# Hybrid SSD and attention trunk in FP32 on one core: order of copies, row splits, down products and weight units at the stage borders

## Chip, cores and metric

The kernel runs on one core of a Trainium2 chip. The metric is the device time in microseconds of one execution, as the median of three runs.

## What is computed

The reference is a bidirectional encoder trunk over 512 positions of width 1024, with two layers. Each layer adds to the residual stream `h`, in this order: half of a SwiGLU feed-forward block (width 2816), a mixer (layer 0: bidirectional Mamba-2 SSD; layer 1: two-dimensional neighbourhood attention), half of a second SwiGLU block, and a gated projection of a per-layer input. Every block normalises `h` first.

```python
def ssd_mixer(h, w_in, conv_w, conv_b, dt_bias, a_log, d_skip, norm_g, w_out):
    proj = h @ w_in
    z, xbc, dt_raw = jnp.split(proj, [SSD_D_INNER, SSD_D_INNER + SSD_CONV_DIM], axis=-1)
    xbc = jax.nn.silu(centred_depthwise_conv(xbc, conv_w, conv_b))
    ...
    y_fwd = ssd_scan(xs, dt[:, :, 0], a[0], grp(b_f), grp(c_f))
    y_bwd = flip(ssd_scan(flip(xs), flip(dt[:, :, 1]), a[1], flip(grp(b_b)), flip(grp(c_b))))
    y = (y_fwd + y_bwd + xs * d_skip[:, None]).reshape(bsz, seqlen, SSD_D_INNER)
    y = rmsnorm(y * jax.nn.silu(z), norm_g)
    return y @ w_out
...
for i in range(DEPTH):
    h = h + 0.5 * swiglu(rmsnorm(h, ffn1_norm[i]), ffn1_w_gu[i], ffn1_w_down[i])
    h = h + mixer_i(rmsnorm(h, mix_norm[i]))
    h = h + 0.5 * swiglu(rmsnorm(h, ffn2_norm[i]), ffn2_w_gu[i], ffn2_w_down[i])
    gate = jax.nn.sigmoid(rmsnorm(h, ple_norm[i]) @ ple_w_gate[i])
    h = h + gate * rmsnorm(p[i] @ ple_w_proj[i], ple_post_norm[i])
```

## The kernel before

The residual stream lies transposed in SBUF, as eight sub-blocks of 128 features by 512 positions (`h[0]` to `h[7]`). Products keep FP32 accuracy by splitting each operand into a rounded high part and the rest: one product is three matmuls, at lines 277, 280 and 281 in `gemm`. A product over eight sub-blocks is 24 matmuls of 512 columns.

**Weights as units.** A unit is a weight tile of 128 by up to 1024, loaded by a DMA (line 204), rounded on ScalarE (line 221, `wh`) and split on DVE (line 223, `wl`), with three buffers each. `plan` lists all units of the program in the order of use. `unit` (line 258) prepares units until three are ready and hands out the first. What `unit` prepares is traced before the product that asked for it.

**Order of the work.** The program text is a priority, not an order: a scheduler at build time issues on each engine what is ready, earlier text first, and hands out the buffers of a ring likewise. `tc.issue_after(ins)` keeps what a block traces on the engine of `ins` behind it.

**FFN.** The first four (in the very first FFN six) column pairs of gate and up are plain products (`gate_up`); the rest are done in blocks of seven products with halves of the columns (`block`, lines 504 to 506, 24 matmuls of 256 columns). `ffn_order` lays the down products of one chunk between the blocks of the next. `activate` multiplies gate and up and splits the result (lines 299 and 300) for the down products. The norm's sum of squares is a column sum on TensorE (`SumSq.begin`, line 342); it is placed inside the second product, after `at` of the eight sub-blocks.

**The first FFN's start.** `first` runs the first four products as loads come in, then prepares three units, and only then (behind the third unit's cast) squares the eight sub-blocks (line 324, ScalarE) and adds them (line 328, DVE).

**SSD.** Eight groups. `project(gi)` makes eight products for a group; the first six go through a convolution of five taps (`conv`: ScalarE lines 748 and 755, DVE lines 752 and 756), the last two are gates (lines 774 and 775). `scan(gi)` is a generator of eight steps that runs beside `project(gi + 1)`, one step per product. Its first step transposes four chunks (line 818), copies them out of PSUM on ScalarE (line 821) and forms the chunk products (line 829), which DVE masks (line 832). All of these use a ring of three PSUM banks (`px_bank`); the big products use a ring of five (`mm_bank`). POOL multiplies the masks in (lines 808 and 811). In the driver, the first product of the next group and its convolution stand in the text ahead of the scan's first step:

```python
for gi in range(NG):
    beside = project(gi + 1) if gi + 1 < NG else out_half()
    sn = scan(gi, *cur, e0)
    ...
    for i, r in enumerate(beside):
        ...
        while pending:
            pending.pop(0)()
        next(sn, None)
```

The last group has no next projection; the first half of the out projection (`out_half`) runs beside it. For this, eight rows of earlier groups come back from DRAM and are scaled and split: cast on ScalarE (line 302), rest on DVE (line 303). Rows 0 to 2 are split beside the last projection, 3 to 7 after the last scan's transposes. `pending` holds a group's gate product (line 926) with its square.

**Attention.** `attend(j)` runs beside `project(j + 1)`. It forms scores (line 1157), transposes the values (line 1191) and the weights (line 1200), and multiplies both (`weigh`, line 1210) into `po`, a bank of the ring of three, which ScalarE and DVE then split (lines 299 and 300).

Of the kernel before, what the change touches and what calls it, by code (L numbers as in the profile page):

```python
# [27 lines left out]
NG = 8  # L28
# [21 lines left out]
def ffn_order(chunks):  # L50

    for f in range(chunks[0][1]):
        yield "plain", f
    for c in range(1, len(chunks)):
        a, b = chunks[c]
        blocks = [(p, i) for p in range(a // 2, b // 2) for i in range(7)]
        d = 0
        for n, (p, i) in enumerate(blocks):  # L60
            yield "block", p, i
            while d < KD and (d + 0.5) * len(blocks) <= KD * (n + 1):
                yield "down", c - 1, d
                d += 1
    yield "between",
    for d in range(KD):
        yield "down", len(chunks) - 1, d
# [3 lines left out]
def trunk(ctx, tc, A, out):  # L71
# [183 lines left out]
        top_up()  # L255
        return True

    def unit():
        while len(ready) < 3 and prep_next():
            pass  # L260
        return ready.pop(0)

# [127 lines left out]
    def ffn(norm, nxt, between=None, first=None, at=4):  # L390
# [159 lines left out]
        for what, *a in ffn_order(chunks):  # L550
            if what == "plain":
                if left and R[0] is not None:
                    sums(left.pop(0))
                gate_up(a[0])
            elif what == "block":

                if between and a in ([chunks[-1][0] // 2, 0], [NF // 2 - 1, 4]):
                    next(between)
                block(*a)
            elif what == "between":  # L560
                made = between and next(between)
            else:
                c, d = a
                last = c == len(chunks) - 1
                pt = mm_bank() if last else px_bank()
                gemm(pt, unit(), [mids[f] for f in range(*chunks[c])])
                v.scalar_tensor_tensor(out=h[d], in0=pt, scalar=0.5, in1=h[d], op0=ALU.mult, op1=ALU.add)
                if last:
                    nxt(d)
                    if d in (2, 4) and made is not None:  # L570
                        made[d // 2]()
# [36 lines left out]
    def ple(l, norm, pp, nxt):  # L608
        halves = (slice(0, T // 2), slice(T // 2, T))

        def gate(n, pt, R, cs):
            if isinstance(pp[n], tuple):
                p_, r3 = pp[n]
                tc.keep_in_program_order(
                    v.scalar_tensor_tensor(out=p_, in0=p_, scalar=col(C_GQ + 8 * l + n), in1=r3, op0=ALU.mult,
                                           op1=ALU.mult))
                pp[n] = p_
            u = t2()[:, cs]
            v.tensor_mul(out=u, in0=pt, in1=R[:, cs])
            s.activation(out=u, in_=u, func=AF.Tanh)  # L620
            v.scalar_tensor_tensor(out=u, in0=u, scalar=1.0, in1=pp[n][:, cs], op0=ALU.add, op1=ALU.mult)
            v.tensor_add(out=h[n][:, cs], in0=h[n][:, cs], in1=u)

        R = None
        for n in range(KD):
            if n == KD - 1 and nxt is done:

                w = unit()
                for x, cs in enumerate(halves):
                    pt = mm_bank()  # L630
                    gemm(pt[:, cs], w, norm.pairs, cols=cs)
                    gate(n, pt[:, cs], R, cs)
                    (sy, s)[x].dma_start(out=out[:, n, cs], in_=h[n][:, cs])
                continue
            pt = mm_bank()
            gemm(pt, unit(), norm.pairs, behind=n == 0)
            if n == 0:
                norm.begin(half=True)
                held = pt
                continue  # L640
            if n == 1:
                R = norm.end()
                gate(0, held, R, slice(0, T))
                nxt(0)
            for cs in ((slice(0, T),) if n < KD - 1 else halves):
                gate(n, pt[:, cs], R, cs)
            nxt(n)


    def ssd(norm, nxt):  # L650
# [107 lines left out]
        def project(gi):  # L758
            bt, ct_, xt, zt = md(), md(), md(), md()
            cts = (16 + gi, 32 + gi, 24 + gi, 40 + gi, 2 * gi, 2 * gi + 1)  # L760
            dsts = (bt[:, 0], bt[:, 1], ct_[:, 0], ct_[:, 1], xt[:, 0], xt[:, 1])
            for i in range(8):
                raw = gi == 0 and i < 3
                if gi == 0 and i == 0:
                    pt = pt0
                else:
                    pt = mm_bank()
                    gemm(pt, unit(), norm.pairs if raw else xn)
                if i < 6:
                    conv(pt, cts[i], dsts[i], raw)  # L770
                else:

                    th = t2()
                    s.activation(out=th, in_=pt, func=AF.Tanh, scale=0.5)
                    v.scalar_tensor_tensor(out=zt[:, i - 6, :], in0=th, scalar=1.0, in1=pt, op0=ALU.add, op1=ALU.mult)
                yield bt, ct_, xt, zt
# [202 lines left out]
                held_[k] = md(F32R)  # L979
                rows[k] = row(k, held_[k])  # L980

        held_ = {}

        def pairs_of(ks):
            res = []
            for k in ks:
                pr = held_.pop(k) if k in held_ else md(F32R)
                yt = row(k, pr) if k < 14 else late[k - 14]
                split(pr, yt, col(C_SN + k))
                res.append(pr)  # L990
            return res

# [16 lines left out]
        for gi in range(NG):  # L1009
            beside = project(gi + 1) if gi + 1 < NG else out_half()  # L1010
            sn = scan(gi, *cur, e0)
            if gi == NG - 1:
                next(sn)
                prs += pairs_of(range(3, 8))
                next(sn)
            for i, r in enumerate(beside):
                cur = r
                if i == 7 and gi == NG - 2:
                    prs = pairs_of(range(3))
                while pending:  # L1020
                    pending.pop(0)()
                next(sn, None)
                if i == 5 and gi == NG - 2:
                    early_rows()
                if i == 6 and gi + 1 < NG:
                    e0 = expo(gi + 1, 0)
# [1 line left out]
        prs = pairs_of(range(8, 16))  # L1028
        ss.begin(0.5, 4.0 * EPS)
        for d in range(KD):  # L1030
            pt, w = mm_bank(), unit()
            gemm(pt, w, prs[:4], last=False)
            if d == 0:
                r2 = ss.end()
            old = sc()
            sy.dma_start(out=old, in_=hd[d])
            gemm(pt, w, prs[4:], first=False, off=4)

            h[d] = hs()
            u = t2()  # L1040
            grid = "p (r c) -> p r c"
            by_column = h[d].rearrange("p (c r) -> p r c", c=64)
            if d < KD - 1:
                v.tensor_add(out=u, in0=pt, in1=parts[d])
                v.tensor_mul(out=u, in0=u, in1=r2)
                v.tensor_add(out=by_column, in0=old.rearrange(grid, c=64), in1=u.rearrange(grid, c=64))
            else:

                v.tensor_mul(out=u, in0=parts[d], in1=r2)
                v.tensor_add(out=by_column, in0=old.rearrange(grid, c=64), in1=u.rearrange(grid, c=64))  # L1050
                w = t2()
                v.tensor_mul(out=w.rearrange("p (c r) -> p r c", c=64), in0=pt.rearrange(grid, c=64),
                             in1=r2.rearrange(grid, c=64))
                v.tensor_add(out=h[d], in0=h[d], in1=w)
            nxt(d)


    def attention(norm, nxt):
# [87 lines left out]
        def attend(j):  # L1146
# [71 lines left out]
            for x in range(2):  # L1218
                turn(2 * x)
                turn(2 * x + 1)  # L1220
                yield
            po = px_bank()
            weigh(po)
            op = opr[j] = md(F32R)
            split(op, po, None)
# [26 lines left out]
        for d in range(KD):  # L1252
            if d < 4:
                pt, w = outs[d]
                gemm(pt, w, opr[6:], first=False, off=6)
            else:
                pt = mm_bank()
                gemm(pt, unit(), opr)
            fetch(d, hd[d])
            v.tensor_add(out=h[d], in0=pt, in1=h[d])  # L1260
            nxt(d)
# [41 lines left out]
    def first(pts, pairs):  # L1303
        done_ = [0] * 4
        here, cut_ = 0, [0] * 4
        for o in order:
# [4 lines left out]
            for u in range(4):  # L1311
                while done_[u] < min(here, 4 * cut_[u]):
                    k = done_[u]
                    gemm(pts[u], begun[u][2:], pairs[k:k + 1], first=k == 0, last=k == KD - 1, off=k)
                    done_[u] += 1
        while len(ready) < 3:
            prep_next()

        with tc.issue_after(splits[-1].ins):
            for k in range(KD):  # L1320
                n.count(k, True)

    for i in range(stop):
        l, w = divmod(i, 4)
# [1 line left out]
        m = None if last else Norm(gains[i + 1], (lambda: md(F32R)) if w == 2 else xa)  # L1326
        nxt = done if last else m.prep
        if w == 0:
            ffn(n, nxt, first=first if i == 0 else None, at=7)
        elif w == 1:  # L1330
            (ssd if l % 2 == 0 else attention)(n, nxt)
        elif w == 2:
            pp = ffn(n, nxt, ple_proj(l))
        else:
            ple(l, n, pp, nxt)
# [103 lines left out]
```

## Time and profile before

| | us |
|---|---|
| runs: median (lowest to highest) | 2330.28 (2328.69 to 2330.52) |
| profiled execution, its own time | 2331.44 |
| span of the profiled execution | 2329.6 |
| TensorE matmuls, busy | 2310.9 (99%) |
| DVE busy | 1827.4 (78%) |
| ScalarE busy | 1166.6 (50%) |
| POOL busy | 323.1 (14%) |

PE is TensorE, ACT is ScalarE, PEld is the load of weights into TensorE, and SP issues the DMAs. Lines are those of the kernel before. In a list of waits each row gives who waited, for what, the sum in us, how many times, and the longest. In a timeline a row gives start, duration of the run of equal instructions, engine, line, operation, tiles and count, and in brackets the idle time before it and what ended it. In windows a row gives the stretch, its length, busy time with the count of instructions, the granted clock of TensorE as a share of full speed, and the share of the DMA engines with GB/s. TensorE's matmuls are pipelined, and their ends in the trace are modelled.

### The profile page before, as it was taken

Reading aid. Unit: us, or ns where it says so; the run is one execution under the profiler, and the core shown is the slowest. Engines: PE = TensorE matmul, PEld = TensorE weight load, DVE = VectorE, ACT = ScalarE, POOL = GpSimd, SP = SyncE. Lnnn points to the kernel's source line nnn. Section 1 sums busy time; section 2 is a strip of 40 time slices with the busy share of each in tenths; the row PEclk is TensorE's granted clock in tenths of the full one; section 3 lists DMA queues with packets and bytes.
Section 4 is the critical chain, followed back from the end, with each engine's and each line's share of the span. In section 5 each row is a group of like instructions: output and inputs, shape, how many; then the busy total and the mean of one; then the engine's idle time right before and its main releaser. Section 6 shows DMA issues by size and latency. Waiting matters only on the chain.

```text
span 2329.6 us, 35378 instructions
## 1 busy us (share of the span) xinstructions
PE 2310.9 (99%) x13798; PEld 2022.4 (87%) x13798; DVE 1827.4 (78%) x2621; ACT 1166.6 (50%) x2028; POOL 323.1 (14%) x253
## 2 busy tenths in 40 slices
PE   9999999999999999999999999999999999999999
PEld 7899998888888788899998889999878788999987
DVE  7878878888877858978875897887678859877856
ACT  5434345776666763543345444334436754343452
POOL 0000001355555551000003100000100010000020
PEclk9999999999999999999999999999999999999999
DMA  5323323444444543223323322332433233323232
GB/s 183 123 73 109 106 88 128 141 145 154 142 148 142 161 160 122 92 95 105 123 69 105 109 84 98 105 123 64 145 120 122 106 114 101 109 100 100 82 100 73
DMA packets 99240, 265.97 MB, mean 114 GB/s; under 512 B 12016, under 2 KB 12912, under 8 KB 99072
## 3 DMA queue, kind: packets, MB, share of 16 engines
q1 hardware_dynamic: 98784, 263.57, 34.3%
q8 instruction: 108, 1.77, 0.3%
q14 instruction: 60, 0.49, 0.1%
q10 hardware_dynamic: 288, 0.14, 0.0%
HBM read 253.40 MB, written 10.26 MB: 113 GB/s over the span
## 4 chain that ended last, share of the span: by engine, by line
PE 63%; DVE 1%; ACT 1%; issue 0%; DVEq 0%; ACTq 0%
PE ps L277 12%; PE ps L280 12%; PE ps L281 12%; PE ps L506 8%; PE ps L505 8%; PE ps L504 8%; PE ps L1210 1%; PE ps L1200 1%; PE ps L1191 0%; PE ps L352 0%; PE ps L1132 0%; PE ps L1157 0%; PE ps L1087 0%; PE ps L342 0%; ACT md L299 0%; DVE md L300 0%
## 5 line engine op out<-in xcount | busy, mean ns | idle before, releaser
L277 PE MATMUL ps<-md,wh 128*128 128x512 f32 (+1 forms) x2032 | 801.5, 395 | 2.0 <-ACT md L299 1.6
L280 PE MATMUL ps<-md,wh 128*128 128x512 f32 (+1 forms) x2032 | 794.4, 391 | 1.1 <-DVE md L303 1.0
L281 PE MATMUL ps<-md,wl 128*128 128x512 f32 (+1 forms) x2032 | 792.0, 390 | 1.7 <-DVE wl L223 1.7
L221 ACT CAST wh<-wr 128x1024 fp32r<-128x1024 f32 (+2 forms) x395 | 352.3, 893 | 528.5 <-issue 195.8
L223 DVE TENSOR_TENSOR wl<-wr,wh 128x1024 fp32r<-128x1024 f32 (+2 forms) x395 | 420.6, 1065 | 85.8 <-ACT wh L221 84.8
L281 PEld LDWEIGHTS ps<-md,wl 128*128 128x128 f32 x2032 | 381.7, 188 | 83.0 <-DVE wl L223 3.1
L277 PEld LDWEIGHTS ps<-md,wh 128*128 128x128 f32 x2032 | 382.3, 188 | 78.6 <-issue 2.4
L280 PEld LDWEIGHTS ps<-md,wh 128*128 128x128 f32 x2032 | 382.4, 188 | 76.5 <-issue 2.8
L221 ACT CAST wh<-md 128x1024 fp32r<-128x1024 f32 x175 | 183.5, 1049 | 318.4 <-PE ps L505 271.8
L328 POOL TENSOR_TENSOR sq<-sq,sq 128x512 f32<-128x512 f32 x71 | 102.7, 1446 | 1703.9 <-ACT sq L324 1699.3
L506 PE MATMUL ps<-sc,wl 128*128 128x256 f32 x980 | 277.4, 283 | 0.0
L506 PE MATMUL ps<-md,wl 128*128 128x256 f32 x980 | 277.3, 283 | 0.0
L505 PE MATMUL ps<-md,wh 128*128 128x256 f32 x980 | 277.3, 283 | 0.0
L505 PE MATMUL ps<-sc,wh 128*128 128x256 f32 x980 | 277.2, 283 | 0.0
L504 PE MATMUL ps<-md,wh 128*128 128x256 f32 x980 | 277.1, 283 | 0.0
L504 PE MATMUL ps<-sc,wh 128*128 128x256 f32 x980 | 276.6, 282 | 0.0
L510 DVE TENSOR_TENSOR t<-ps,t 128x512 f32<-128x512 f32 x245 | 165.7, 688 | 126.3 <-PE ps L506 123.8
L223 DVE TENSOR_TENSOR wl<-md,wh 128x1024 fp32r<-128x1024 f32 x175 | 213.5, 1220 | 22.3 <-ACT wh L221 22.1
L505 PEld LDWEIGHTS ps<-sc,wh 128*128 128x128 f32 x980 | 187.7, 192 | 4.0
L504 PEld LDWEIGHTS ps<-sc,wh 128*128 128x128 f32 x980 | 187.7, 192 | 3.8
L504 PEld LDWEIGHTS ps<-md,wh 128*128 128x128 f32 x980 | 188.0, 192 | 1.4
L505 PEld LDWEIGHTS ps<-md,wh 128*128 128x128 f32 x980 | 188.0, 192 | 1.4
(212 smaller groups left out, 2896.5 us busy)
## 6 DMA issues: line engine op xcount, KB each, us to landing
wr<-in_w_gw_dram SPq DMA_DIRECT2D x70, 512.0 KB, 3.6
md<-in_w_gw_dram SPq DMA_DIRECT2D x70, 512.0 KB, 5.2
wr<-in_w_in_dram SPq DMA_DIRECT2D x65, 512.0 KB, 3.5
wr<-in_w_dn_dram SPq DMA_DIRECT2D x128, 256.0 KB, 2.7
wr<-in_w_gu_dram SPq DMA_DIRECT2D x32, 512.0 KB, 3.5
hs<-crow SPq DMA_DIRECT2D x64, 256.0 KB, 3.8
wr<-in_w_dn_dram SPq DMA_DIRECT2D x32, 384.0 KB, 3.1
wr<-in_w_qkv_dram SPq DMA_DIRECT2D x24, 512.0 KB, 3.5
```

The lines of the kernel that those rows point to most:

```text
L221: splits.append(s.copy(out=hi[:, :n], in_=raw[:, :n]))
L223: v.tensor_sub(out=lo[:, :n], in0=raw[:, :n], in1=hi[:, :n])
L277: m = te.matmul(out=pt, lhsT=hi[:, sl], rhs=part(xp, 0, cols), start=first and k == 0, stop=False)
L280: te.matmul(out=pt, lhsT=hi[:, sl], rhs=part(xp, 1, cols), start=False, stop=False)
L281: te.matmul(out=pt, lhsT=lo[:, sl], rhs=part(xp, 0, cols), start=False, stop=last and k == n - 1)
L328: (v if fast else g).tensor_add(out=self.acc, in0=self.acc, in1=q)
L504: te.matmul(out=o, lhsT=hi[:, sl], rhs=xh, start=j == 0 and kk == 0, stop=False)
L505: te.matmul(out=o, lhsT=hi[:, sl], rhs=xl, start=False, stop=False)
L506: te.matmul(out=o, lhsT=lo[:, sl], rhs=xh, start=False, stop=j == 1 and kk == 3)
L510: v.tensor_add(out=k[to], in0=pt, in1=k[other])
L1200: te.transpose(out=pp[:, i * P:(i + 1) * P], in_=x[:, i * P:(i + 1) * P], identity=ident)
L1210: te.matmul(out=po[a * 64:(a + 1) * 64, b * P:(b + 1) * P], lhsT=vk[:, 2 * b + u, a * 64:(a + 1) * 64], rhs=y[:, i * P:(i + 1) * P], start ...
```

## The change

1. In `ffn_order`, the down products of a chunk are laid between the blocks half a step later.
2. `unit(last)` prepares nothing ahead when the product is the last of its stage (FFN, gated projection, SSD, attention).
3. In SSD, a projection stops once more after its first product, so that the scan's first step (transposes, copies, chunk products) is traced ahead of the first convolution.
4. In the last group all eight rows are split after the first part of the scan's first step, and the ScalarE part of the pending gate product is queued behind the last row's cast.
5. In attention the product `po` takes a bank of the ring of five.
6. At the start one unit is prepared ahead of the squares, and the others after them. Layer 1's first FFN places the sum of squares after six sub-blocks, not seven.

```diff
@@ ffn_order
-            while d < KD and (d + 0.5) * len(blocks) <= KD * (n + 1):
+            while d < KD and (d + 1) * len(blocks) <= KD * (n + 1):
@@ unit
-    def unit():
-        while len(ready) < 3 and prep_next():
+    def unit(last=False):
+
+        while (not last or not ready) and len(ready) < 3 and prep_next():
             pass
         return ready.pop(0)
@@ ffn
-                gemm(pt, unit(), [mids[f] for f in range(*chunks[c])])
+                gemm(pt, unit(last and d == KD - 1), [mids[f] for f in range(*chunks[c])])
@@ ple
-            gemm(pt, unit(), norm.pairs, behind=n == 0)
+            gemm(pt, unit(n == KD - 1), norm.pairs, behind=n == 0)
@@ ssd, project
                     gemm(pt, unit(), norm.pairs if raw else xn)
+                if gi and i == 0:
+                    yield
                 if i < 6:
                     conv(pt, cts[i], dsts[i], raw)
@@ ssd, pairs_of
-        held_ = {}
+        held_, row_cast = {}, []
...
-                split(pr, yt, col(C_SN + k))
+                row_cast[:] = [split(pr, yt, col(C_SN + k))]
@@ ssd, the groups
             if gi == NG - 1:
                 next(sn)
-                prs += pairs_of(range(3, 8))
-                next(sn)
+                prs = pairs_of(range(8))
+            else:
+                next(beside)
+
+            next(sn)
             for i, r in enumerate(beside):
                 cur = r
-                if i == 7 and gi == NG - 2:
-                    prs = pairs_of(range(3))
+                if pending and gi == NG - 1:
+                    with tc.issue_after(row_cast[0].ins):
+                        pending.pop(0)()
                 while pending:
                     pending.pop(0)()
-                next(sn, None)
+                if i or gi == NG - 1:
+                    next(sn, None)
...
-            pt, w = mm_bank(), unit()
+            pt, w = mm_bank(), unit(d == KD - 1)
@@ attention
-            po = px_bank()
+            po = mm_bank()
...
-                gemm(pt, unit(), opr)
+                gemm(pt, unit(d == KD - 1), opr)
@@ first
-        while len(ready) < 3:
-            prep_next()
+        prep_next()
 
         with tc.issue_after(splits[-1].ins):
             for k in range(KD):
                 n.count(k, True)
+        while len(ready) < 3:
+            prep_next()
@@ the loop over stages
-            ffn(n, nxt, first=first if i == 0 else None, at=7)
+            ffn(n, nxt, first=first if i == 0 else None, at=6)
```

## Rows read from the trace of the kernel before

**Rows 1.** The page, part 1: busy time of the engines.
```profile
PE 2310.9 (99%) x13798; PEld 2022.4 (87%) x13798; DVE 1827.4 (78%) x2621; ACT 1166.6 (50%) x2028; POOL 323.1 (14%) x253
```

**Rows 2.** Timeline of TensorE, 533 to 544 us.
```profile
533.49 1.47 PE L818 MATMUL ps<-msk,md 128*128 128x128 f32 x12
...
539.59 0.39 PE L277 MATMUL ps<-md,wh 128*128 128x512 f32 x1
539.82 0.39 PE L280 MATMUL ps<-md,wh 128*128 128x512 f32 x1
540.63 0.66 PE L818 MATMUL ps<-msk,md 128*128 128x128 f32 x4 [0.42 <-ACT md L821]
...
542.92 0.48 PE L281 MATMUL ps<-md,wl 128*128 128x512 f32 x1
```

**Rows 3.** Waits of TensorE, 470 to 800 us.
```profile
PE ps L818 <- ACT md L821: 4.5, 6, 2.4
```

**Rows 4.** Waits of TensorE, 800 to 822 us.
```profile
PE ps L818 <- ACT md L821: 1.7, 1, 1.7
PE ps L280 <- DVE md L303: 1.0, 2, 0.7
```

**Rows 5.** Waits of TensorE, 0 to 60 us.
```profile
PE ps L342 <- DVE sq L328: 1.2, 1, 1.2
```

**Rows 6.** Waits of TensorE, 1290 to 1400 us.
```profile
PE ps L277 <- ACT md L299: 1.6, 1, 1.6
```

**Rows 7.** Instructions of line 1191, whole span: idle before them until (us, times).
```profile
  DVE md L300: 2.8, 7
```

**Rows 8.** Windows of TensorE; the column behind the count is the granted clock.
```profile
484.00:488.00 4.00, 4.00 (x22) 0.65 0.07 25
811.00:815.00 4.00, 3.90 (x21) 0.57 0.14 45
```

**Rows 9.** Timeline of TensorE, 480 to 488 us.
```profile
483.41 1.12 PE L818 MATMUL ps<-msk,md 128*128 128x128 f32 x4 [2.36 <-ACT md L821]
...
487.23 0.48 PE L281 MATMUL ps<-md,wl 128*128 128x512 f32 x1
```

**Rows 10.** Timeline of ScalarE, 533 to 544 us.
```profile
534.77 0.77 ACT L748 ACTIVATE t<-ps,ccw 128x512 f32<-128x512 f32 x1
539.47 0.63 ACT L755 ACTIVATE t<-t 128x512 f32<-128x512 f32 x1 [3.93 <-DVE t L752]
540.01 2.03 ACT L821 COPY md<-ps 128x512 f32<-128x512 f32 x4
```

**Rows 11.** Timeline of ScalarE, 18 to 30 us.
```profile
19.01 1.05 ACT L221 CAST wh<-wr 128x1024 fp32r<-128x1024 f32 x1 [2.64 <-DMA wr<-in_w_gu_dram]
```

**Rows 12.** Timeline of ScalarE, 803 to 821 us.
```profile
807.12 2.02 ACT L302 ACTIVATE md<-t,cst 128x512 fp32r<-128x512 f32 x3 [2.06 <-DMA t<-ydram]
...
810.46 1.07 ACT L821 COPY md<-ps 128x512 f32<-128x512 f32 x2
```

**Rows 13.** Timeline of DVE, 803 to 821 us.
```profile
807.88 2.08 DVE L303 SCALAR_TENSOR_TENSOR md<-t,cst,md 128x512 fp32r<-128x512 f32 x3 [1.20 <-ACT md L302]
...
815.52 4.14 DVE L303 SCALAR_TENSOR_TENSOR md<-t,cst,md 128x512 fp32r<-128x512 f32 x3
```

**Rows 14.** Timeline of POOL, 803 to 821 us.
```profile
815.74 1.67 POOL L808 TENSOR_TENSOR sc<-sc,sc 128x512 f32<-128x512 f32 x1 [1.47 <-DVE sc L832]
```

**Rows 15.** Timeline of DVE, 18 to 32 us.
```profile
24.04 5.47 DVE L328 TENSOR_TENSOR sq<-sq,sq 128x512 f32<-128x512 f32 x7
```

**Rows 16.** Window of TensorE over one block of layer 1's first FFN.
```profile
1364.45:1367.30 2.85, 2.85 (x25) 1.00 0.19 72
```

**Rows 17.** Timeline of TensorE, 1325 to 1330 us.
```profile
1328.17 1.01 PE L342 MATMUL ps<-ones_d,sq 128*128 128x1 f32 x8
```

**Rows 18.** Timeline of DVE, 1321 to 1330 us.
```profile
1322.97 1.55 DVE L223 TENSOR_TENSOR wl<-wr,wh 128x1024 fp32r<-128x1024 f32 x1
...
1327.32 0.69 DVE L328 TENSOR_TENSOR sq<-sq,sq 128x512 f32<-128x512 f32 x1
```

## The prediction

> **What bounds the kernel.** I read the page first: TensorE is busy 99% of the span [rows 1]. So the matmul stream is the bound, and a change that removes no matmul (this one removes none) can only win where that stream stands still. The busy share hides most of that. In the timeline of TensorE a 512-column matmul is booked with 0.39 us, but the next one starts 0.23 us later [rows 2]. A pause in the stream is therefore the booked idle time plus 0.16 us that the modelled end covers; I count each wait as idle + 0.16.
>
> The waits of TensorE, asked for stretch by stretch, list what is to be had. In SSD's middle the transposes L818 wait for ScalarE's copies L821, 4.5 us in six times [rows 3]. In SSD's last group they wait 1.7 us for the same copies, and the out gemm 1.0 us for the row splits L303 [rows 4]. At the start it is 1.2 us for the sum of squares L328 [rows 5], in layer 1's first FFN 1.6 us for the cast L299 [rows 6]. In attention the weight loads of the value transposes L1191 wait 2.8 us in seven times for the product's split L300 [rows 7].
>
> A second loss is no idle time at all. The windows by granted clock show 0.65 and 0.57 of full speed right after the two longest pauses [rows 8], that is a fall to the lower of the two levels (1.2 GHz). Its cost: four transposes and sixteen chunk products take from 483.41 to the next gemm at 487.23, 3.82 us [rows 9]; the same twenty at full clock take from 540.63 to 542.92, 2.29 us [rows 2]. The difference is 1.5 us, twice.
>
> **SSD's copies ahead of the convolution.** Before, ScalarE's queue at a border holds the convolution's identity, its tanh and then the four copies. The tanh waits 3.93 us for the four DVE taps and the copies stand behind it until 540.01 [rows 10], although their transposes were issued at 533.49 [rows 2]. Transposes and chunk products share three PSUM banks, so the fourth chunk's transposes wait for the first copy. After the change the copies stand ahead of the convolution in program order and claim their buffers first. No instruction is added. What comes later is the convolution, its taps and tanh by up to the four copies, 2.03 us [rows 10]; its result is read by the next group's scan, one border later (483.41 [rows 9] to 540.63 [rows 2], 57 us), so nothing waits. Gain: 4.5 + 6 x 0.16 + 1.5 of clock = 7.0 us. I keep back 0.2 us a border, 1.2 in all, because a weight cast of 1.05 us [rows 11] can still come ahead of the copies. I take 5.8; ends 3.5 and 7.0.
>
> **Last group: rows after the copies.** Here no gemm can fill in, because the out projection needs the split rows. Before, three row casts wait for their loads until 807.12 and hold ScalarE; the copies come at 810.46 [rows 12]. After, the copies come first, and all eight casts and their DVE splits follow. At stake: 1.7 + 1.0 idle, 0.5 hidden (three waits), 1.5 of clock, together 4.7 us. What is late next are the splits: six of them must pass DVE while the out gemm wants one per 0.68 us (three matmuls). Three took 2.08 us at 807.88, but 4.14 us at 815.52 [rows 13], while POOL ran a masked product of 1.67 us [rows 14]. After the change more of the splits run while POOL is busy. At 0.69 each the gemm is not held; at 1.38 six of them cost 6 x 0.7 = 4.2 us, nearly all of it. I take 2.7, between the two because some run before POOL's products start; ends -0.5 and 4.7. The Square tied behind the last cast feeds only the sum over all sixteen rows, which is read after the whole first half of the out projection: nothing.
>
> The Trainium skill (SBUF — State Buffer, section "Who interferes with whom") states that a DVE instruction with two SBUF inputs and a GpSimd instruction that reads SBUF use one port, and that the later one waits until the other is through. The slow splits agree with it. By that rule alone every split could wait for a whole POOL product, the last group would gain nothing, and the time would be 2321.7.
>
> **Attention.** The product's bank moves from the ring of three to the ring of five. Before, the next value transposes need the bank that DVE's split of the product still reads: 2.8 us in seven times [rows 7]. The other users of the ring of three release earlier, so the wait goes unless the scores' own release takes its place. The ring of five has room: at most four open output sums and this product. I take 1.9; ends 1.0 and 2.8.
>
> **Start.** The squares queue behind the first weight cast, which ends at 20.06 [rows 11], no longer behind the third. DVE's seven adds take 5.47 us [rows 15]; begun at 21.3, after two squares, they end near 26.8, where now they end at 29.5. TensorE waited 1.2 us for them [rows 5], so 2.7 is more than enough. The two weight splits that move behind the adds fit into what is left. At stake 1.2 + 0.16; I take 1.2; ends 0.5 and 1.3.
>
> **FFN order.** The first down product of a chunk comes after two blocks, not one. A block is some 25 matmuls in 2.85 us [rows 16], more than the 1.6 us wait of layer 1's first FFN [rows 6]. But DVE is packed there, and the second block's weights become late next. I take 1.2; ends 0.4 and 1.8. No other FFN shows this wait, and there the move is free: every down product still follows within a block.
>
> **Sum of squares at 6 instead of 7.** It starts at 1328.17 [rows 17], right behind the add that runs 0.69 us from 1327.32 [rows 18]. Three matmuls earlier it would wait some 0.5 us, and win part of that back at the factor. I take -0.3; ends -0.6 and +0.3.
>
> **Borders without units ahead.** One unit per border is traced after the last sub-block's chain. But the engines' queues go by readiness: at 1322.97 a unit's split of 1.55 us [rows 18] stands ahead of the gate's product, though it is traced behind it. The same unit goes into the same gap: 0; ends -0.8 and +0.8.
>
> **Sum.** 5.8 + 2.7 + 1.9 + 1.2 + 1.2 - 0.3 = 12.5. A new order can bring a new wait; one like that at the start, 1.2 [rows 5], I set against it: 11.3. The profiled execution took 2331.44 us, so 2320.1; the median of the runs shown, 2330.28, is 1.16 lower, which gives 2319.0. About 0.2% (4.7 us) is what a measurement of this kernel can tell from no change.
>
> **Rivals.** First, the waits form again: the copies go early, but the transposes then wait for the next thing (the mask products' banks, the row splits), and the clock falls all the same. For it speak the slow splits [rows 13]; against it that the five later borders pause only 0.4 us each. Attention, start, FFN and a third of the rest remain: 1.9 + 1.2 + 1.2 - 0.3 + 2.8 - 1.2 = 5.6, hence 2324.7, and with one more wait 2325.9. Chance 0.15.
>
> Second, slower: the units are really late. If a border's second unit is cut only behind the last sub-block's chain, then after layer 0's gates its cast begins at about 1327.2 (the last add starts at 1327.32 [rows 18]) and ends 1.05 us later, at 1328.2, with the split still to come. The first unit's 21 matmuls, counted back from 1328.17 [rows 17], end at 1323.3. TensorE would wait 4.9 us, and 1.5 more if the clock falls: 6.4. With half of that at the six other borders, 25.6 us against a gain of 11.3: 2344.6. It decides from 2.3 us a border on (16 in all: the gain and 4.7). Against it stands the split at 1322.97, which did not wait for its turn in the text. Chance 0.08.
>
> Third, the change doesn't do what it says: readiness undoes the order of the text for SSD's copies too, and only the bank and the start win, 3.1 us: 2327.2. Chance 0.05; the copies' claim on buffers speaks against it.
>
> **How the numbers follow.** The forecast has 0.72; its terms' ends don't fall together, and give it 2313.5 to 2324.5. To leave out no more than 2 in 10 the range reaches over the first rival to 2327. Faster by over 0.2% is below 2325.6: the forecast and half of the first rival, 0.80. Within 0.2%: the rest of that and the third, 0.12. Slower: 0.08.
>
> **What would show it.** Right: L818 waits for L821 under 1.5 us over all seven borders; no window of SSD at the lower clock; on ScalarE the copies ahead of the tanh; no weight load of L1191 waiting for L300; L342 without a wait near 28. Wrong: a wait of 2 us or more in a new place, above all gemms behind L223 right after a border, or row splits that hold the out projection longer than 4 us.

## The result, and the profile after

The kernel after takes 2334.85 us in the median (2332.82 to 2336.07, 12 runs), the kernel before in the same session 2330.4 us: a ratio of 1.0021, 95% interval [1.0013, 1.0029]. The change made the kernel 0.2% slower. The forecast was 2319.0 us, the range ended at 2327.0; it was wrong in sign, and no rival named the place where the time was lost.

The page of after shows the same bound as [rows 1], and one digit that is new: the granted clock, in tenths of full speed, has an 8 late in the span. From here on, lines are those of the kernel whose profile is shown.

```profile
PE 2312.0 (99%) x13798; PEld 2027.6 (87%) x13798; DVE 1823.6 (78%) x2621; ACT 1175.2 (50%) x2028; POOL 311.7 (13%) x253
...
PEclk9999999999999999999999999999998999999999
```

To find where the time went I matched every instruction of TensorE with its twin in the profile before (the n-th of its source line) and took the difference of the two starts, as a median over the 15 us from the time given. Minus is earlier than before. This is worked out from one profiled execution of each kernel (not rows of a view), and the kernels of the experiments below stand beside after; the last column is the difference of the spans (2333.7 - 2329.6 = 4.1 us).

```
start minus start before, us   60    420    780    840   1305   1335   1395   1725    end
after                       -1.02  -1.16  -0.90  -3.78  -3.82  -2.78  -3.76  -4.00  +4.05
b_po_mm                     -1.29  -1.34  -2.86  -3.26  -3.28  -3.26  -3.26  -3.23  +4.16
a_po_px                     -1.54  -1.68  -2.92  -5.92  -5.94  -4.91  -5.88  -6.12  -6.10
a_po_first                  -0.99  -1.12  -2.42  -5.36  -5.41  -2.78  -3.80  -4.04  +1.66
a_po_own                    +2.18  +9.48  +2.69  -0.30  -0.33  +2.31  +1.27  +3.21  +5.95
b_copies                    -1.32  -1.35  -2.73  -4.78  -4.79  -4.78  -4.77  -4.77  -4.64
b_last                      -1.07  -1.11  -2.75  -5.52  -5.52  -5.50  -5.51  -5.48  -5.39
c_px_at7                    -1.29  -1.39  -1.10  -4.08  -4.11  -3.37  -4.15  -4.39  -4.34
c_px_split                  -1.37  -1.50  -8.43 -11.40 -11.44 -10.68 -11.44 -11.68 -11.64
c_units                     -0.53  -0.69  -7.65 -10.66 -10.70 -10.69 -11.45 -11.69 -11.60
c_start                     -0.83  -0.98  -7.93 -10.93 -10.97 -10.23 -10.99 -11.23 -11.23
c_order                     -2.22  -2.22  -9.15 -12.14 -12.12 -11.37 -11.38 -11.34 -11.23
```

The first line, read as steps: by 1725 us the kernel is 4.0 us ahead, 2.9 of them won in SSD's last group (780 to 840) and 1.0 before 60 us. SSD's other groups (420 to 780) lose 0.3. The norm of layer 1's first FFN (1305 to 1335) loses 1.0, its first chunk border wins 1.0 back. Then attention loses 8.05 us, twice the whole lead.

The waits of TensorE in after, 1740 to 1770 us; in before the same view of 1740 to 1774 us is empty:

```profile
PE ps L1165 <- ACT md L1200: 2.6, 1, 2.6
PE ps L1165 <- DVE sc L1175: 2.2, 1, 2.2
PE ps L1208 <- ACT md L1200: 0.9, 1, 0.9
PE ps L1140 <- DVE sc L1175: 0.3, 1, 0.3
```

L1165 are the scores of head 0, L1175 the softmax's first step, L1200 the copy of the value transposes. And the windows of after, by granted clock (span, busy and count of PE, PEld, DVE, ACT and POOL, then the clock):

```profile
1740.00:1751.45 11.45, 8.15 (x51) 6.30 (x49) 10.15 (x24) 6.65 (x11) 0.00 (x0) 1.00 0.89 315
1751.45:1765.11 13.66, 10.97 (x58) 9.11 (x60) 9.30 (x37) 8.54 (x26) 0.00 (x0) 0.50 0.29 97
```

After the two long waits TensorE runs 13.66 us at the lower level (1.2 GHz). In before the clock is 1.00 all through that work (1744.00 to 1769.11 us). TensorE's timeline of after shows what stands in its queue there:

```profile
1746.78 0.40 PE L282 MATMUL ps<-md,wl 128*128 128x512 f32 x1
1749.77 0.97 PE L1165 MATMUL ps<-md,hs 64*128 64x256 f32 x6 [2.59 <-ACT md L1200]
1752.92 1.65 PE L1165 MATMUL ps<-md,hs 64*128 64x256 f32 x6 [2.18 <-DVE sc L1175]
1754.49 1.12 PE L1199 MATMUL ps<-msk,t 128*128 128x128 f32 x4
1755.90 1.84 PE L1140 MATMUL ps<-msk,sc 128*128 128x2 f32 x8 [0.28 <-DVE sc L1175]
...
1767.05 0.47 PE L278 MATMUL ps<-md,wh 128*128 128x512 f32 x1
```

From 1747.2 to 1767.05 us there is no dense product (L278 to L282) at all: head 0's scores, softmax, turns (the transposes of the weights) and weighing stand bare, without a product to fill their waits. The order of TensorE's instructions in the two traces says the same. Counts from head 0's first scores on; Q is the product right behind po in the text (the second one of projection 2), P the one right ahead of it, R the one after Q:

```
before: scores 12, values, P 6, Q 18, scores 6, Q 4, scores 6, Q 2, values, R 4, query sums, R 17, turns 8, ...
after:  scores 12, values, P 6, scores 12, values, query sums, turns 16, weigh 32, scores 12, values, Q 4, ...
```

The other waits of after, which answer to [rows 3], [rows 4], [rows 5] and [rows 6], by window 470 to 800, 800 to 822, 15 to 60 and 1290 to 1400 us:

```profile
PE ps L821 <- ACT md L824: 4.1, 6, 1.9
```

```profile
PE ps L281 <- DVE md L304: 0.7, 1, 0.7
PE ps L821 <- ACT md L824: 0.2, 1, 0.2
PE ps L832 <- ACT md L824: 0.2, 1, 0.2
```

```profile
PE ps L282 <- DVE wl L223: 0.6, 1, 0.6
```

```profile
PE ps L343 <- DVE sq L329: 1.2, 1, 1.2
PE ps L505 <- ACT wh L221: 0.4, 1, 0.4
PE ps L282 <- DVE wl L223: 0.3, 1, 0.3
```

So SSD's waits, the largest term, stayed nearly whole (4.1 of 4.5 us); the last group's went from 2.7 to 1.1 us; the wait at the start is gone; the cast's wait in layer 1's FFN is smaller, and a new one stands ahead of it (L343). The value transposes (L1199, whole span) no longer wait for the product's split, which took 2.8 us in [rows 7]; what is left is a wait for the softmax:

```profile
  DVE sc L1175: 0.4, 2
```

### The profile page after: what moved, and what is told of

It is laid out like the page before. It is cut to its first block, busy times and chain, and to the rows that moved or that the text cites. A ratio compares the mean times of both kernels' runs of the same rounds, so it can differ in the third digit from the quotient of the medians.

```text
span 2333.7 us, 35377 instructions
## 1 busy us (share of the span) xinstructions
PE 2312.0 (99%) x13798; PEld 2027.6 (87%) x13798; DVE 1823.6 (78%) x2621; ACT 1175.2 (50%) x2028; POOL 311.7 (13%) x253
## 4 chain that ended last, share of the span: by engine, by line
PE 60%; DVE 4%; ACT 1%; issue 0%; DVEq 0%; ACTq 0%
PE ps L278 11%; PE ps L281 11%; PE ps L282 11%; PE ps L507 8%; PE ps L506 8%; PE ps L505 8%; DVE wl L223 1%; PE ps L1218 1%; PE ps L1208 1%; PE ps L1165 0%; PE ps L1095 0%; PE ps L1199 0%; DVE md L304 0%; PE ps L343 0%; DVE sc L1175 0%
## 5 line engine op out<-in xcount | busy, mean ns | idle before, releaser
L278 PE MATMUL ps<-md,wh 128*128 128x512 f32 (+1 forms) x2032 | 802.6, 395 | 0.0
L282 PE MATMUL ps<-md,wl 128*128 128x512 f32 (+1 forms) x2032 | 790.8, 389 | 1.6 <-DVE wl L223 1.6
L282 PEld LDWEIGHTS ps<-md,wl 128*128 128x128 f32 x2032 | 381.7, 188 | 83.6 <-DVE wl L223 2.9
L278 PEld LDWEIGHTS ps<-md,wh 128*128 128x128 f32 x2032 | 382.5, 188 | 75.6 <-issue 2.6
```

Source lines behind the costliest of these rows:

```text
L278: m = te.matmul(out=pt, lhsT=hi[:, sl], rhs=part(xp, 0, cols), start=first and k == 0, stop=False)
L282: te.matmul(out=pt, lhsT=lo[:, sl], rhs=part(xp, 0, cols), start=False, stop=last and k == n - 1)
```

## The experiments

All kernels were timed against the kernel before, whose medians in these sessions were 2329.83 to 2330.3 us.

**Attention.** Theory A: TensorE's order is laid down when the program is built, and a ring gives its banks out in the order of the text (px is the ring of three, mm the ring of five). In the text po stands between P and Q. With po in mm, Q can't be placed ahead of head 0's weighing. Theory B puts the loss down to the other edits, C to head 0's cold start, D to the scores being freed by an emptier ring px. The first kernel undoes the edit alone:

```diff
-            po = mm_bank()
+            po = px_bank()
```

> The kernel after with the product's bank of weigh taken back from the ring px; all else as after. Theory A, the ring's order: a ring hands its banks out in the order of the text, so with po in the ring mm every dense product that stands behind po in the text has to stand behind head 0's weigh in TensorE's queue too, and the scores of head 0 lose their cover. Then attention comes back to its shape of before, the 8.06 us lost between 1743 us and the end are gone, and the time is 2334.85 - 8.06 = 2326.8 us, with no stretch at half clock after 1740 us. Theory B, the loss comes from another part of the change (the units left out at the borders, or the order in layer 1's feed-forward), which attention meets at its start: 2334 to 2336 us, the waits of 2.6 and 2.2 us still there.

Measured: 2325.89 us (ratio 0.9984 [0.9976, 0.9993]). The line of a_po_px in the table keeps its lead through attention (-6.12 to -6.10), and the view of TensorE's waits from 1740 to 1770 us is empty. B is out. The second kernel is before with only this edit:

> The kernel before with po moved to the ring mm and nothing else. Theory A: head 0's scores stand bare as in the kernel after, 2330.4 + 8.06 = 2338.5 us (2337 to 2340), half clock for some 13 us at attention's start. Theory B, and the prediction's own term for this edit: the six waits of 0.35 us go and nothing comes, 2328.5 us.

Measured: 2337.55 us, ratio 1.0034 [1.0022, 1.0045]. Its waits, 1740 to 1774 us, are those of after (line numbers of before):

```profile
PE ps L1157 <- ACT md L1192: 2.6, 1, 2.6
PE ps L1157 <- DVE sc L1167: 1.7, 1, 1.7
PE ps L1200 <- ACT md L1192: 0.9, 1, 0.9
PE ps L1132 <- DVE sc L1167: 0.3, 1, 0.3
```

From 1725 us to the end it loses 7.4 us. This one line, alone, makes the kernel slower by more than the whole change does. The third kernel tells A from C:

```diff
-            po = mm_bank()
+            po = px_bank() if j == 0 else mm_bank()
```

> The kernel after with po in px for head 0 alone and in mm for heads 1 to 7. Theory A, the ring's order: the dense products that run ahead are now stopped behind head 1's po instead, so the pile of scores, transposes and weigh without products between moves on to head 1: the time stays near after's, 2331 to 2335 us, and the long waits stand some 15 us later. Theory C, it is head 0's cold start alone (the keys' factors just made, the table load on ScalarE, the first biases) that makes the bank's place costly: 2334.85 - 8.06 - some of the 1.9 us of the six waits = 2325 us, no wait over 1 us after 1743 us.

Measured: 2331.24 us (1.0009 [1.0, 1.0018]). The pile has moved by one head, as A says; head 1 is no colder than the others, yet 5.7 us are lost. Waits of TensorE, 1740 to 1790 us:

```profile
PE ps L1208 <- ACT sc L1190: 1.6, 2, 1.2
PE ps L1199 <- DVE md L301: 1.3, 1, 1.3
PE ps L1140 <- ACT md L1200: 0.9, 1, 0.9
PE ps L1165 <- ACT md L1200: 0.7, 1, 0.7
PE ps L1208 <- DVE sm L1179: 0.4, 1, 0.4
```

C is out. The fourth gives po a bank that nobody else queues for. The Trainium skill (PSUM — Partial Sum Buffer, section "Specifications (TRN2)") counts eight banks per partition; no run here tests that number, but the kernel's two rings hold five and three, so I cut mm by one.

```diff
-            po = mm_bank()
+            po = bank("po", 1)
...
-    mm_bank = lambda: bank("mm", 5)
+    mm_bank = lambda: bank("mm", 4)
```

> The kernel after with po in a ring of its own of one bank, and the ring mm cut from 5 banks to 4, everywhere in the kernel. Theory A, the ring's order: no product stands behind po and no transposes of the values stand behind it either, so both losses are gone: 2326.8 less the six waits of 0.35 us = 2324.8 us, plus whatever four banks cost the other stages (0 to 3 us). Theory D, what hurts is not the ring mm but that the ring px, with po out of it, lets a head's scores and transposes run together ahead of the products: the waits at attention's start stay, 2333 to 2336 us.

Measured: 2336.01 us (1.0026 [1.0015, 1.0036]). By the time alone that is D's number. The trace says otherwise: no wait on scores or softmax stands between 1740 and 1790 us, and none of the value transposes waits for po. What costs is in the main the shorter ring elsewhere. Waits of TensorE, 1640 to 1790 us, where the only one listed is the keys' products waiting for a bank:

```profile
PE ps L278 <- DVE md L1091: 2.0, 2, 1.3
```

The table shows the rest: 2.2 us behind before by 60 us, 3.2 by 1725, where after is 4.0 ahead. D is out for attention's start. So is want of room: with only four banks for the products, 24 of their matmuls follow head 0's first scores, as in before. Yet attention still loses 2.7 us (3.21 to 5.95), with no more than 0.4 us of waits of TensorE after 1740 us; why is open. That a bank of its own would pay if there were a ninth is not shown.

**SSD and the last group.** Theory E, that the wait forms again, comes from ScalarE's timeline of after at a border. The copies now come ahead of the convolution (L749), as planned. But a weight cast stands ahead of them, and the fourth block of transposes follows the third at once:

```profile
533.11 1.05 ACT L221 CAST wh<-wr 128x1024 fp32r<-128x1024 f32 x1
534.07 2.02 ACT L824 COPY md<-ps 128x512 f32<-128x512 f32 x4
535.97 0.80 ACT L749 ACTIVATE t<-ps,ccw 128x512 f32<-128x512 f32 x1
```

And TensorE's, where twelve transposes run into the other four with nothing between them, while in [rows 2] a whole product of 24 matmuls stood there:

```profile
532.79 1.47 PE L821 MATMUL ps<-msk,md 128*128 128x128 f32 x12
534.69 0.66 PE L821 MATMUL ps<-msk,md 128*128 128x128 f32 x4 [0.43 <-ACT md L824]
535.18 2.04 PE L832 MATMUL ps<-md,md 128*128 128x128 f32 x16
```

The wait is 0.43 us as it was 0.42 [rows 2]: the release is 6 us earlier, and so is the instruction that needs it. The kernel before with this part alone:

```diff
+                if gi and i == 0:
+                    yield
                 if i < 6:
                     conv(pt, cts[i], dsts[i], raw)
...
+            else:
+                next(beside)
+            next(sn)
...
-                next(sn, None)
+                if i or gi == NG - 1:
+                    next(sn, None)
```

> The kernel before with SSD's copies put ahead of each later group's first convolution, and nothing else of the change. The prediction: the waits in front of the fourth block of transposes go, 2330.4 - 5.8 = 2324.6 us. Theory E, the wait re-forms: before, the second product's 24 matmuls stood between the third and the fourth block of transposes; with the copies early the fourth block follows the third at once, and its bank is free only when the first copy has ended, so each of the six borders keeps some 0.59 us, the scan of the first group gains a wait of 1.3 us, and only the clock's fall near 485 us may go: 2328 to 2331 us.

Measured: 2327.52 us (0.9993 [0.9984, 1.0002], not told from no change). Six waits of 4.0 us remain in 470 to 800 us. Its lead over before from 420 to 780 us (1.38 us) is not this part's: the next kernel, which doesn't have it, shows 1.64 there, because the clock didn't fall near 485 us in either. The 2.1 us won in the last group, which the expectation had left out, are not its copies' either: their wait grew from 1.7 us [rows 4] to 2.5, and the clock fell there too (0.86 over 804 to 816 us). What went is the products' wait for the row splits: three of them fell into a gap of POOL (810.04 to 812.56 us) and took 2.08 us, where [rows 13] had 4.14. Waits of TensorE, 800 to 822 us, and DVE's timeline of b_copies:

```profile
PE ps L820 <- ACT md L823: 2.5, 1, 2.5
```

```profile
810.77 2.08 DVE L303 SCALAR_TENSOR_TENSOR md<-t,cst,md 128x512 fp32r<-128x512 f32 x3
```

The last group alone:

```diff
-                prs += pairs_of(range(3, 8))
+                prs = pairs_of(range(8))
...
-                if i == 7 and gi == NG - 2:
-                    prs = pairs_of(range(3))
+                if pending and gi == NG - 1:
+                    with tc.issue_after(row_cast[0].ins):
+                        pending.pop(0)()
```

> The kernel before with the last group's row splits and gate product in the fixed order, and nothing else of the change; the copies of the last group stay where they were. The prediction's term: 2330.4 - 2.7 = 2327.7 us, with the half clock near 811 us gone. Theory F, the gain at 806 to 820 us in the kernel after (2.9 us) came from the copies ahead of the last group's first product, not from the rows: 2330 us.

Measured: 2325.9 us (0.9985 [0.9977, 0.9994]); 2.8 us won between 780 and 840 us. The term was right, and F is out. Then the mechanism of E, on the kernel with po in px and seven pairs (which is told below): the first product of a group is cut in two, so that twelve matmuls stand between the third block of transposes and the fourth.

```diff
+                    if gi and i == 0:
+                        u0 = unit()
+                        gemm(pt, u0, xn[:4], last=False)
+                        yield
+                        gemm(pt, u0, xn[4:], first=False, off=4)
+                        yield
...
             for c in range(NC):
+                if c == 3 and gi < NG - 1:
+                    yield
                 pt = px_bank()
...
                 next(beside)
+                next(sn)
+                next(beside)
```

> As the kernel before it in this list (po in px, seven pairs), and in SSD the first product of each later group is cut in two: its first four pairs, then the first three blocks of transposes with their copies, then its last four pairs (12 matmuls, 2.7 us), then the fourth block. Theory E: the six waits of 0.59 us in front of the fourth block are gone, 2324.9 - 3.5 = 2321.4 us. Rival H, the copies on ScalarE are the bound there whatever stands between, so the wait moves to the next bank's user (the fourth block or the products of B and C): 2324.9 us.

Measured: 2319.78 us, ratio 0.9959 [0.9947, 0.9972], 5.9 us under the kernel it builds on. Waits of TensorE, 470 to 800 us, and ScalarE at one border:

```profile
PE ps L828 <- ACT md L831: 0.2, 1, 0.2
```

```profile
526.61 1.56 ACT L831 COPY md<-ps 128x512 f32<-128x512 f32 x3 [3.09 <-PE ps L828]
...
530.00 1.05 ACT L221 CAST wh<-wr 128x1024 fp32r<-128x1024 f32 x1 [0.90 <-PE ps L281]
530.96 0.58 ACT L831 COPY md<-ps 128x512 f32<-128x512 f32 x1
```

E is borne out and H is out: ScalarE had been free, it copies at once, and the cast comes later. The gain is larger than the 3.5 us I expected, because one of the six waits, the first border's, was 1.9 us and goes too; the six sum to 4.1 us, 5.1 with 0.16 hidden in each. From 420 to 780 us the kernel wins 6.9 us, of which 1.6 is the clock that held, the part that b_last shows without any edit there.

**The small parts.** Seven pairs in place of six:

```diff
-            ffn(n, nxt, first=first if i == 0 else None, at=6)
+            ffn(n, nxt, first=first if i == 0 else None, at=7)
```

> The kernel after with po back in px, and layer 1's first feed-forward back at seven pairs ahead of the norm's sum (2325.89 us without the second edit). Theory G, six pairs don't cover the sum of squares: the wait of 1.39 us at 1321 us goes, and 1.0 us is gained (up to 2.6 where the clock fell there): 2324.9 us (2323.3 to 2325.2). The prediction's term has it the other way: six pairs are worth 0.3 us, so 2326.2 us.

Measured: 2325.67 us (0.9985 [0.9976, 0.9993]), no different from 2325.89. The wait shrinks to 0.5 us and doesn't go; G had its size wrong. From 1305 to 1335 us the loss is 0.74 us, where a_po_px has 1.03: six pairs cost 0.3 us. In two kernels with six pairs (a_po_first, a_po_own) that stretch costs 2.6 us. For a_po_first the window shows the clock down (count, clock):

```profile
1318.00:1328.00 10.00, 8.77 (x36) 0.83 0.45 157
```

The other 0.7 us is the units, as the next kernel shows; it prepares them at the borders as before:

```diff
-                gemm(pt, unit(last and d == KD - 1), [mids[f] for f in range(*chunks[c])])
+                gemm(pt, unit(), [mids[f] for f in range(*chunks[c])])
...
-            gemm(pt, unit(n == KD - 1), norm.pairs, behind=n == 0)
+            gemm(pt, unit(), norm.pairs, behind=n == 0)
```

(and likewise at the output projections of SSD and attention).

> The kernel with po in px, seven pairs and SSD's product cut in two (2319.78 us), with the units at the four kinds of stage border prepared ahead as in the kernel before. The prediction's term: 0 either way, 2319.8 us. Theory I, read from where the traces part: with the edit the norm of layer 1's first feed-forward waits 0.7 us longer at 1316 us, and 0.13 us at 345 and 0.24 us at 1635 us are gained, so undoing it gives 2319.8 - 0.3 = 2319.5 us, with the wait of 0.7 us at the border to layer 1 gone.

Measured: 2319.17 us (0.9954 [0.9942, 0.9967]). The wait for the sum of squares is gone and nothing is lost from 1305 to 1335 us, but the 0.13 and 0.24 us that I had also put down to this edit stay; they belong to the FFN order (c_order loses them). This is the fastest version seen, 0.5% under before; its lead over c_px_split, 0.6 us, is within what the runs scatter. The start as before:

```diff
-        prep_next()
+        while len(ready) < 3:
+            prep_next()
         with tc.issue_after(splits[-1].ins):
```

> The same kernel (2319.78 us) with the start's order as before: all three units prepared ahead of the first norm's sum of squares. The prediction's term: the wait of 1.2 us near 28 us comes back, 2321.0 us. Theory J, that wait stands in the one profile of before alone (kernels with the start unchanged show none of it in other runs), so the edit is worth nothing: 2319.8 us.

Measured: 2320.2 us (0.9962 [0.9949, 0.9974]). The wait near 28 us doesn't come back, nor is it there in b_last, b_copies or b_po_mm, which all have the start of before. Waits of TensorE, 15 to 60 us, of b_last:

```profile
PE ps L281 <- DVE wl L223: 0.7, 1, 0.7
```

The last one puts the FFN's down products where they were:

```diff
-            while d < KD and (d + 1) * len(blocks) <= KD * (n + 1):
+            while d < KD and (d + 0.5) * len(blocks) <= KD * (n + 1):
```

> The same kernel (2319.78 us) with the feed-forward's down products placed as before (half a place earlier). The prediction's term: 1.2 us, so 2321.0 us and the wait of 1.8 us on a split pair near 1362 us back. By where the traces part, 0.7 us: 2320.5 us.

Measured: 2320.77 us (0.9963 [0.9949, 0.9976]). The old wait is back (1290 to 1400 us):

```profile
PE ps L278 <- ACT md L300: 1.6, 1, 1.6
PE ps L343 <- DVE sq L329: 0.5, 1, 0.5
```

By the table the order is worth 0.8 us there and 0.3 at 1635 us.

## Why the prediction was wrong, step by step

- **Attention, +1.9: the step that failed.** It looked at the ring that po leaves (px) and at the ring's room ("at most four open output sums and this product"), and set both ends of the bound above zero. What it took off was right: the seven waits went, worth 0.35 us of stream each for six and 0.2 for one, 2.3 us. It never asked who stands behind po in the ring that po enters. Those are the dense products, TensorE's only cover for a softmax chain. They had run about a projection ahead of head 0; with po in their ring they can't run further. Price: 6.0 us of waits (6.6 with 0.16 hidden in each of the four) and the clock. The net loss is 8.05; with the 2.3 us won, 10.4 were lost, so about 4 us (3.8 to 4.4) are left for the clock and its 13.66 us at the lower level. This last figure is a difference, not measured by itself. Rows of after give a higher estimate: the weighing of one head took 3.15 us at the lower level and 1.97 at full clock, and half of the 10.97 us booked at 0.50 is 5.5 us. How the loss splits between waits and clock is thus known to some 2 us only.

```profile
1762.65 3.15 PE L1218 MATMUL ps<-sc,md 128*64 128x128 f32 x32
...
1780.02 1.97 PE L1218 MATMUL ps<-sc,md 128*64 128x128 f32 x32
```

- **SSD's copies, +5.8: mechanism half right, gain not there.** The copies did move ahead of the tanh, by 6 us. The step took the instruction that waits (the fourth transposes) as fixed and only its releaser as moved. But the transposes were placed behind a product because the copies were late; with the copies early they were placed at once. From 420 to 780 us after loses 0.26 us (the clock fell near 480 us in it as in before), and b_copies against b_last gives the same 0.26. The weight cast that the step held back 0.2 us for did come ahead of the copies. The first group's scan also got a wait of 1.2 us on POOL's masked products, the one new wait I had counted. The first rival (waits re-form) is what happened in this part.
- **Last group, +2.7: right.** 2.9 in after, 2.8 alone. The splits were slow as feared, but not to the end of the bound: five took 5.65 us, 1.13 each between 0.69 and 1.38, with POOL busy all along. POOL is slowed too: six of its products took 5.71 us there, and in b_copies, with DVE nearly idle, the same six 3.47.

```profile
810.23 5.65 DVE L304 SCALAR_TENSOR_TENSOR md<-t,cst,md 128x512 fp32r<-128x512 f32 x5
812.23 5.71 POOL L848 TENSOR_TENSOR sc<-md,md 128x256 f32<-128x256 f32 x6
```

The rule of the Trainium skill (SBUF — State Buffer, section "Who interferes with whom") says which engines hold each other up; the prediction read it as a wait for a whole POOL product at every split, and then the part would have won nothing. The measurement decides: the splits are slowed, and 2.9 us are left.

- **Start, +1.2: nothing.** The term was read from a wait that one execution had. Other executions of the same code don't have it, so the run, not the edit, took it away. By 60 us the four kernels with the old start lead the profile of before by 0.8 to 1.3 us, those with the new one by 0.5 to 2.2 (a_po_own with its shorter ring left aside).
- **FFN order, +1.2: right**, 1.0 in after, 0.8 alone (c_order), and some 0.3 more at two later places. **Six pairs, -0.3: right**, but for the clock, which fell in two of four such profiles. **Borders, 0: -0.7** at layer 1, within its ends; the split that stood ready in [rows 18] did not go into the same gap: it began at 1320.22 us, 1.07 later than its place in before (1322.97) less the lead of 3.82.

Together: without attention the change is worth 4.0 us in the profile, 1.0 of it from the start, where the edit did nothing. The signs of what to look for had the right kind of loss ("a wait of 2 us or more in a new place"), but looked for it at the borders and the row splits, and the chance of 0.08 for slower rested on the units at the borders, the only mechanism I had looked for. Of the ring that po moves into only the room was asked for, not the order.

## What to carry to other kernels

A buffer's ring is also a queue: before a tile moves to another ring, list what stands behind it in that ring in the order of the text, and what work that holds back, not only whether there is room. When a releaser is moved earlier, ask whether the waiting instruction moves with it; if nothing is placed between the two, the wait goes along, and a piece of independent work put there by hand (half a product) removes it. A wait found in one execution is a term only if other executions of the same code show it.

## What the runs showed of the hardware

The granted clock near 480 us differs from execution to execution in code that is the same there: the profile of before fell to the lower level, b_po_mm, identical up to attention, did not. Windows of TensorE, first of before, then of b_po_mm (busy, count, clock):

```profile
476.00:488.00 12.00, 9.64 (x46) 0.86 0.45 154
```

```profile
476.00:488.00 12.00, 9.65 (x53) 1.00 0.52 175
```

TensorE is booked busy for the same time in both, but it got through 46 matmuls in the one and 53 in the other; the fall is worth 1.6 us (b_last, 420 to 780 us). It fell in after (0.86) and not in a_po_px (1.00), which are the same code there. A term for the clock taken from one profile is thus a chance, not a sum. The second surprise is the length: after two waits of 2.59 and 2.18 us the lower level lasted 13.66 us, through 10.97 us of booked work with pauses of 0.28 and 0.94 us in it, where the falls in [rows 8] followed one pause and cost 1.5 us. In a_po_first, with waits of 4.9 us in all and none above 1.3, the clock stayed at 1.00 from 1760 to 1772 us and was 0.79 over the 8 us after.
